# Four more tokens leave the dense expert tables and are gathered: 96 + 4 gathered, 160 to 156 dense

## The chip, the cores and the metric

One core of a Trainium2 chip runs the kernel. The metric is device time in microseconds; the figure shown of a kernel is the median of its runs.

## The reference, cut to what matters

A block over 256 tokens of width 2048: dilated attention and a three-branch sparse attention, a memory cross attention, and at the end a mixture over 16,384 small experts (PEER). Only the mixture and the last norm are touched here:

```python
eid = e1 * N_KEYS + e2
g = jax.nn.softmax(vs, axis=-1)
a = jax.nn.gelu(jnp.einsum('nd,ned->ne', xb, u_tab[eb]))
y = jnp.einsum('ne,ned->nd', a * gb, v_tab[eb])
h = h + y ; out = rmsnorm(h, norm_final)
```

Both tables `u_tab` and `v_tab` are 16384 x 2048 float32, 134 MB each.

## The kernel before, in words

`phase1` computes everything up to the first part of the query projection of the mixture. `phase2` is the mixture, and the change lies in it.

Tokens are handled in two ways. The first `NA` = 160 tokens are **dense**: both tables are streamed whole through TensorE, every expert is multiplied with all of these tokens, and a weight matrix that is zero where an expert wasn't chosen picks out what counts. Tokens 160 to 255 are **gathered**: an indirect DMA of GpSimd (POOL) fetches the 128 rows of a table that 128 partitions name, 1 MB a gather. `GROUPS` gives their layout: tokens 192 to 255 sit on 64 partitions, two copies of them, so that two experts of a token are fetched by one gather and 64 gathers do for a table; tokens 160 to 191 sit on 32 partitions, four copies, 32 gathers a table.

Order of the work:
- `route`, `give`, `gates` and `turned` find the experts and softmax weights, beside the query projection; `give` brings expert numbers and weights of the gathered tokens into the partition layout of their group by a matmul with a 0/1 matrix (`rep`), one quarter at a time (`b` = 0 to 3). `spread` builds the dense weight matrix from one-hot matmuls (`gp`, lines 1077 to 1105), one turn for four dense tokens, one turn in each tick.
- First table: 32 x 8 loads of 512 KB (line 1205) over the SP queue into eight buffers; a load feeds 8 matmuls of 128 x 128 by `NA` columns (line 1213), which the profile shows as 16 PE instructions, since float32 takes two each. In the text such a load with its matmuls is a **unit**.
- Second table: again 256 loads (line 1248) with 8 matmuls each (line 1242), summing into six PSUM banks over all 128 blocks of experts. The matmuls of blocks 126 and 127 are held back for the end (`close`).
- Gathers: the list `steps` holds them in order. `gtick` (line 1058) is called once a unit and moves on in the list by `RATE` = 0.415 steps a unit in the first table; at unit 256 the rate is set so that what is left is spent over 250 units of the second. Nine steps and the first are already done before, by `early` (line 1126) and line 1150. `paced` (line 985) ties each gather to the matmul that was the last when it was listed, so POOL goes no faster than TensorE. `fetch` takes one of four buffers `ga`; when three more are under way VectorE uses a fetched tile: `dot` (line 1010) against the token's row, `add` (line 1020) into the sum `acc`.
- `fold` (line 1030) adds up the copies of group 0 while the second table still runs: four matmuls of `acc` with a 0/1 matrix (line 1041) into two spare PSUM banks and four additions (line 1036). Group 1 is added up at the end, in `turn` (line 1280), which also transposes the dense result; then norm and output.

Tile orders each engine's instructions; TensorE, VectorE, ScalarE and POOL each work through their own queue in that order.

Of the kernel before, what the change touches and what calls it, by code (L numbers as in the profile page):

```python
# [26 lines left out]
A_SLOPES = [float(np.float32(2.0 ** (-8.0 * (i + 1) / 12))) for i in range(12)]  # L27
B_SLOPES = [float(np.float32(2.0 ** (-8.0 * (i + 1) / 16))) for i in range(16)]
ROW_NAMES = ("norm_mix", "norm_x", "norm_mem", "norm_ffn")
NA = 160  # L30
GROUPS = ((192, 64, 2), (160, 32, 4))
NE1 = 76
NPF = 7
GA = 4
LAG = 3
RATE = 0.415
SYNC = mybir.DependencyInfo(mybir.DependencyClass.Sync, mybir.DependencyReason.DATA)


# [814 lines left out]
def phase2(c):  # L854
    nc, I, pool = c.nc, c.I, c.pool
    g_s2, sp = pool("s2")
    g_ga, gap = pool("ga")
    g_w, wp = pool("wt")
    wta = wp.tile([128, NE1, NA], F32, name="wta")
    flat = wta[:].rearrange("p e n -> p (e n)")  # L860
    g_q, qp = pool("rt", side="right")
    skp = Banks(c.pp, ["s0", "s1"])
    up = Banks(c.pp, ["b0", "b1", "b2", "b3", "tr", "pv"])

    eT = [sp.tile([128, NA], F32, name=f"eT{i}") for i in range(3)]
    state = {"E": 0, "N": 0, "wtb": None, "unit": 0, "g": 0.0, "rate": RATE, "early": 0, "done": 0}
    selm = sp.tile([128, len(GROUPS), 128], F32, name="selm")
    nc.gpsimd.dma_start(selm[:], I["sel"])
    identr = qp.tile([128, 128], R, name="identr")
    nc.scalar.copy(identr[:], c.ident[:])  # L870
    sk = qp.tile([128, 2, 128], F32, name="sk")
    nc.gpsimd.dma_start(sk[:], I["sub_keys"])
    repk = qp.tile([128, sum(k for _, _, k in GROUPS), 128], F32, name="repk")
    nc.gpsimd.dma_start(repk[:], I["rep"])
    grp = []
    o = 0
    for gi, (t0, n, k) in enumerate(GROUPS):
        cc = 128 // k
        grp.append({"t0": t0, "n": n, "k": k, "cc": cc, "sum": selm[:, gi, :],
                    "rep": [repk[:, o + j, :] for j in range(k)],  # L880
                    "idx": sp.tile([128, cc], U32, name=f"idx{gi}"), "gate": sp.tile([128, cc], F32, name=f"gate{gi}"),
                    "a": sp.tile([128, cc], F32, name=f"a{gi}"), "rs": sp.tile([128, 1], F32, name=f"rs{gi}")})
        o += k
    v = qp.tile([128, 2, 16, 16], F32, name="v")
    ix = qp.tile([128, 2, 16, 16], U32, name="ix")
    ixk = qp.tile([128, 2, 16, 16], U32, name="ixk")
# [51 lines left out]
    def gates(hf, hs):  # L938

        n = hs.stop - hs.start  # L940
        gs = qp.tile([128, 2, 8], F32, name="gs")
        g3 = efs[hf][:, 2, 16 * hs.start:16 * hs.stop].rearrange("p (a c) -> p a c", c=16)
        v3 = vs[:, hf, hs, :]
        nc.vector.tensor_sub(g3, v3, v3[:, :, 0:1].to_broadcast([128, n, 16]))
        yield
        yield
        nc.scalar.activation(g3, g3, AF.Exp)
        yield
        nc.vector.reduce_sum(gs[:, 0, 0:n], g3, axis=AX.X)
        nc.vector.reciprocal(gs[:, 1, 0:n], gs[:, 0, 0:n])  # L950
        nc.vector.tensor_mul(g3, g3, gs[:, 1, 0:n][:, :, None].to_broadcast([128, n, 16]))

    def give(b):

        ef = efs[1]
        sl = slice(32 * b, 32 * b + 32)
        nc.vector.scalar_tensor_tensor(ef[:, 3, sl], ef[:, 0, sl], 128.0, ef[:, 1, sl], ALU.mult, ALU.add)
        yield from gates(1, slice(2 * b, 2 * b + 2))
        for _ in range(LAG):
            yield  # L960
        for g in grp:
            k, w = g["k"], 32 // g["k"]
            ps = skp.tile([128, 2, w], F32, name="sc")
            for j in range(k):
                nc.tensor.matmul(ps[:], g["rep"][j], ef[:, 2:4, 32 * b + j * w:32 * b + j * w + w],
                                 start=j == 0, stop=j == k - 1)
            nc.scalar.copy(g["gate"][:, b * w:b * w + w], ps[:, 0, :])
            nc.vector.tensor_copy(g["idx"][:, b * w:b * w + w], ps[:, 1, :])
            if b == 0:
                pr = skp.tile([128, 1], F32, name="sc")  # L970
                for j in range(k):
                    nc.tensor.matmul(pr[:], g["rep"][j], c.rsf[:, 1:2], start=j == 0, stop=j == k - 1)
                nc.scalar.copy(g["rs"][:], pr[:])
# [11 lines left out]
    def paced(ins):  # L985

        c.tc.add_manual_dep(ins.ins, c.last_sub.name, SYNC, reason="pace")

    def rows():
# [10 lines left out]
                nc.vector.scalar_tensor_tensor(g["x"][:], g["x"][:], g["rs"][:], gn[:], ALU.mult, ALU.mult)  # L1000
        return norm

    def fetch(g, i, table, use):
        t = gap.tile([128, D], F32, name="ga", tag="ga", bufs=GA)
        paced(nc.gpsimd.indirect_dma_start(out=t[:], out_offset=None, in_=table,  # L1005
                                           in_offset=bass.IndirectOffsetOnAxis(ap=g["idx"][:, i:i + 1], axis=0)))
        return lambda: use(g, i, t)
# [14 lines left out]
    steps = [rows]  # L1022
    for b in range(4):
        for g in grp:
            steps += [lambda g=g, i=i: fetch(g, i, I["ur"], dot) for i in range(b * g["cc"] // 4, (b + 1) * g["cc"] // 4)]
    for g in grp:
        steps += [lambda g=g, i=i: fetch(g, i, I["vr"], add) for i in range(g["cc"])]
    steps.insert(len(steps) - grp[1]["cc"] + 8, lambda: fold(grp[0]))

    def fold(g):  # L1030
# [7 lines left out]

    def share_sums(g, z, nb):
        r = slice(g["t0"] - 128, g["t0"] - 128 + g["n"])  # L1040
        nc.tensor.matmul(z[r, :], g["sum"][:, r], g["acc"][:, nb * 512:nb * 512 + 512], start=True, stop=True,
                         skip_group_check=True)
        return r

    def gathered():
# [93 lines left out]
    for b in range(4):  # L1139
# [58 lines left out]
    o = c.pj.n % 4  # L1198
    up.tags = ["tr", "pv"] + [f"b{(o + i) % 4}" for i in range(4)]
    for b in range(32):  # L1200
        e0 = 4 * b
        ps = [up.tile([128, 512], F32, name="up") for _ in range(4)]
        for u in range(8):
            i = 8 * b + u
            raw = ahead[i] if i < len(ahead) else load(I["u"][b, u])
            for k in range(2):
                kt = 2 * u + k
                x = xr[kt // 6][:, kt % 6, :]
                if b == 0:
# [59 lines left out]
    ss, rs = [fin[:, hf, 0:4] for hf in range(2)], [fin[:, hf, 5:6] for hf in range(2)]  # L1269
    n1 = NA - 128  # L1270
# [9 lines left out]
    def turn(nb):  # L1280
        zt = (spare, tags[0:2], tags[2:4], spare)[nb]
        z = [c.pp.tile([128, 512], F32, name=f"z{h}", tag=zt[h]) for h in range(2)]
        y = [ysb[d // 3][:, d % 3 * NA:d % 3 * NA + NA] for d in range(4 * nb, 4 * nb + 4)]
        for i in range(4):
            nc.tensor.transpose(z[0][:, i * 128:i * 128 + 128], y[i][:, 0:128], c.ident[:])
        for i in range(4):
            nc.tensor.matmul(z[1][0:n1, i * 128:i * 128 + 128], y[i][:, 128:NA], c.ident[:], start=i == 0, stop=True,
                             skip_group_check=True)
        share_sums(grp[1], z[1], nb)
        for hf in range(2):  # L1290
            x = hres[nb][:, hf, :]
            n = 128 if hf == 0 else GROUPS[0][0] - 128
            nc.vector.tensor_add(x[0:n], x[0:n], z[hf][0:n, :])
            nc.scalar.activation(sq[:, hf, :], x, AF.Square, accum_out=ss[hf][:, nb:nb + 1])

    def stat(hf):
# [135 lines left out]
```

## Time and profile before

| what | value |
|---|---|
| median of 3 runs | 2149.53 us (2148.39 to 2154.59) |
| profiled execution, its own time | 2152.23 us |
| its span | 2150.4 us |
| first table's matmuls (line 1213) | 915.8 to 1562.6 us |
| second table's matmuls (line 1242) | 1562.6 to 2135.1 us |
| moved by DMA | 642.15 MB, mean 299 GB/s |

A time is read as: engine busy, idle before, what ended the idle. `PEld` is the weight load of TensorE, beside `PE`, the matmuls. "DMA share" is the mean busy share of the 16 DMA engines, and can read a little over 1. Between the span and the execution's own time lie 1.8 us outside of the first and last instruction.

### The profile page before, as it was taken

The numbers are of one execution on the slowest core, as the hardware profiler recorded it, in microseconds if no ns is written. First come the engines' busy times: TensorE is split into PE (matmuls) and PEld (weight loads), VectorE is DVE, ScalarE is ACT, GpSimd is POOL, SyncE is SP. The second block draws the span as 40 slices with busy tenths as digits, with TensorE's granted clock in tenths as the row PEclk, the third lists the DMA queues.
The fourth block names the chain that finished last, engine by engine and source line by source line (L and its number), as shares of the span: only waits on it lengthen the run. The fifth ranks groups of instructions, "written<-read, shape, count | busy, mean of one in ns | idle before, by whom it ended". The sixth has DMA issues, their size and how long they took to land.

```text
span 2150.4 us, 36374 instructions
## 1 busy us (share of the span) xinstructions
PE 2109.8 (98%) x14602; PEld 1992.1 (93%) x14602; DVE 1236.1 (57%) x2304; ACT 565.3 (26%) x1290; POOL 272.0 (13%) x252
## 2 busy tenths in 40 slices
PE   8999999999999999999999999999999999999997
PEld 7998998777888888989989999999999999998996
DVE  5555655776575656798866666666443333333334
ACT  5454444656545555431101111000000000000001
POOL 0000000000000000132221221222311111111111
PEclk9999999999999999999999999999999999999999
DMA  7566545444655556888999999999999999998994
GB/s 247 177 193 190 166 137 165 147 138 138 195 177 188 186 168 218 262 309 337 397 414 415 407 401 407 405 399 408 414 413 413 412 412 404 400 385 320 397 394 189
DMA packets 152089, 642.15 MB, mean 299 GB/s; under 512 B 16928, under 2 KB 19264, under 8 KB 126960
## 3 DMA queue, kind: packets, MB, share of 16 engines
q1 hardware_dynamic: 120704, 426.06, 54.7%
q0 software_dynamic: 30496, 212.69, 24.8%
q8 instruction: 114, 1.87, 0.4%
q10 hardware_dynamic: 720, 1.08, 0.2%
q14 instruction: 55, 0.45, 0.1%
HBM read 635.57 MB, written 4.19 MB: 298 GB/s over the span
## 4 chain that ended last, share of the span: by engine, by line
PE 80%; issue 9%; DMA 5%; DVE 4%; POOL 2%; ACT 1%; POOLq 0%; DVEq 0%; ACTq 0%
PE up L1213 22%; PE y_b L1242 10%; PE pj L168 7%; PE pj L169 7%; PE pj L170 7%; PE y_s L1242 6%; PE pj L205 5%; PE pj L204 5%; PE pj L203 4%; DMA ga<-in_ur_dram,idx 2%; PE gp L1092 2%; POOL ga L1005 1%; DVE ga L1010 1%; DMA raw<-in_v_dram 1%; PE sc L602 1%
## 5 line engine op out<-in xcount | busy, mean ns | idle before, releaser
L1213 PE MATMUL up<-xr,raw 128*128 128x160 f32 x3968 | 547.3, 299 | 3.1 <-DMA raw<-in_u_dram 3.1
L150 DVE TENSOR_TENSOR wl<-raw,wh 128x512 fp32r<-128x512 f32 (+1 forms) x576 | 391.5, 684 | 268.1 <-ACT wh L149 265.3
L1213 PEld LDWEIGHTS up<-xr,raw 128*128 128x128 f32 x3968 | 540.5, 190 | 3.9 <-DMA raw<-in_u_dram 2.8
L149 ACT CAST wh<-raw 128x512 fp32r<-128x512 f32 (+1 forms) x576 | 352.0, 616 | 409.4 <-PE pj L204 166.4
L1020 DVE SCALAR_TENSOR_TENSOR acc<-ga,a,acc 128x2048 f32<-128x2048 f32 x94 | 221.0, 2352 | 397.6 <-DMA ga<-in_vr_dram,idx 397.6
L1010 DVE SCALAR_TENSOR_TENSOR ga<-ga,gx 128x2048 f32<-128x2048 f32 x96 | 219.9, 2291 | 148.9 <-DMA ga<-in_ur_dram,idx 148.8
L1242 PE MATMUL y_b<-wta,raw 128*128 128x160 f32 x1520 | 219.1, 299 | 0.6 <-DMA raw<-in_v_dram 0.6
L1242 PEld LDWEIGHTS y_b<-wta,raw 128*128 128x128 f32 x1520 | 210.6, 190 | 0.8 <-DMA raw<-in_v_dram 0.8
L1005 POOL DMA_INDIRECT ga<-in_vr_dram,idx x96 | 109.2, 1138 | 522.4 <-PE y_b L1242 440.8
L1005 POOL DMA_INDIRECT ga<-in_ur_dram,idx x96 | 125.8, 1310 | 378.7 <-PE up L1213 124.7
L205 PE MATMUL pj<-nh,wl 128*128 128x256 f32 x576 | 164.1, 285 | 0.0
L204 PE MATMUL pj<-nl,wh 128*128 128x256 f32 x576 | 164.0, 285 | 0.0
L203 PE MATMUL pj<-nh,wh 128*128 128x256 f32 x558 | 160.6, 288 | 0.0
L1242 PE MATMUL y_b<-wtb,raw 128*128 128x160 f32 x1040 | 151.8, 300 | 0.0
L168 PE MATMUL pj<-wh,nh 128*128 128x512 f32 (+1 forms) x384 | 150.2, 391 | 0.6 <-ACT wh L149 0.6
L1242 PEld LDWEIGHTS y_b<-wtb,raw 128*128 128x128 f32 x1040 | 144.6, 190 | 4.4 <-issue 4.4
L1278 ACT COPY ysb<-y_s 128x480 f32<-128x480 f32 x1 | 0.6, 560 | 560.0 <-PE y_s L1242 560.0
L169 PE MATMUL pj<-wl,nh 128*128 128x512 f32 (+1 forms) x384 | 147.2, 383 | 0.2 <-DVE wl L150 0.2
L170 PE MATMUL pj<-wh,nl 128*128 128x512 f32 (+1 forms) x384 | 147.0, 383 | 0.0
L1242 PE MATMUL y_s<-wta,raw 128*128 128x160 f32 x912 | 136.4, 299 | 0.2 <-DMA raw<-in_v_dram 0.2
L1242 PEld LDWEIGHTS y_s<-wta,raw 128*128 128x128 f32 x912 | 128.0, 190 | 0.4 <-DMA raw<-in_v_dram 0.4
L205 PEld LDWEIGHTS pj<-nh,wl 128*128 128x128 f32 x576 | 111.3, 193 | 0.7
(343 smaller groups left out, 2903.6 us busy)
## 6 DMA issues: line engine op xcount, KB each, us to landing
raw<-in_v_dram SPq DMA_DIRECT2D x256, 512.0 KB
raw<-in_u_dram SPq DMA_DIRECT2D x249, 512.0 KB
raw<-in_w_in_dram SPq DMA_DIRECT2D x160, 512.0 KB
raw<-in_w_out_dram SPq DMA_DIRECT2D x32, 512.0 KB
raw<-in_w_pq_dram SPq DMA_DIRECT2D x32, 512.0 KB
raw<-in_w_up_b_dram SPq DMA_DIRECT2D x16, 512.0 KB
raw<-in_w_xkv_dram SPq DMA_DIRECT2D x16, 512.0 KB
raw<-in_w_up_a_dram SPq DMA_DIRECT2D x8, 512.0 KB
```

The source lines that it names most:

```text
L149: c.last_act = nc.scalar.copy(h[:, :cols], raw[:, k, :cols]).ins
L150: c.last_sub = nc.vector.tensor_sub(l[:, :cols], raw[:, k, :cols], h[:, :cols].bitcast(F32)).ins
L168: nc.tensor.matmul(o, xh[:, s], h[:, :cols], start=kt == 0, stop=False)
L169: nc.tensor.matmul(o, xh[:, s], l[:, :cols], start=False, stop=False)
L170: c.last_mm = nc.tensor.matmul(o, xl[:, s], h[:, :cols], start=False, stop=kt == nk - 1).ins
L203: nc.tensor.matmul(o, h[:, s], xh, start=False, stop=False)
L204: nc.tensor.matmul(o, h[:, s], xl, start=False, stop=False)
L205: c.last_mm = nc.tensor.matmul(o, l[:, s], xh, start=False, stop=kt == nk - 1 and j % 2 == 1).ins
L1005: paced(nc.gpsimd.indirect_dma_start(out=t[:], out_offset=None, in_=table, in_offset=bass.IndirectOffsetOnAxis(ap=g["idx"][:, i:i + 1], ax ...
L1010: nc.vector.scalar_tensor_tensor(t[:], t[:], 1.0, g["x"][:], ALU.mult, ALU.mult, accum_out=g["a"][:, i:i + 1])
L1213: c.last_mm = c.last_sub = nc.tensor.matmul(ps[j][:, 0:NA], raw[:, k, j * 128:j * 128 + 128], x, start=kt == 0, stop=kt == KT - 1).ins
L1242: c.last_mm = c.last_sub = nc.tensor.matmul(o, raw[:, d // 4 % 2, d % 4 * 128:d % 4 * 128 + 128], wt, start=e == 0 and d % 3 == 0, stop=e ...
```

## The change

Tokens 156 to 159 leave the dense part (`NA` = 156) and are gathered as a third group, `four`: 4 tokens on 32 partitions each, so 4 gathers a table (128 partitions a gather, 32 experts of each token). Its rows `x` and its sum `acc` don't lie in one tile of 128 x 2048 but in four of 128 x 512, in buffers of the projection that are free by then. `give` gets a third layout step; `four_rows` loads the rows of the four tokens by 16 DMAs, each of which spreads 512 elements of one token over 32 partitions, and the gain row by one. `four_dot` and `four_add` do the work of `dot` and `add` in four pieces. In the list of steps, `four_rows` and the 4 gathers of the first table come behind the other 96, the 4 gathers of the second behind the first 8 of group 0, and a second `fold` stands five steps ahead of the first one. The rate in the first table goes from 0.415 to 0.395. In `turn` the second half's addition becomes two (partitions 0 to 27 and 32 to 63).

```diff
-NA = 160
+NA = 156
 GROUPS = ((192, 64, 2), (160, 32, 4))
+FOUR = 156
...
-RATE = 0.415
+RATE = 0.395
...
+    four = {"t0": 128, "n": 32, "cc": 4, "sum": selm[:, len(GROUPS), :], "rep": repk[:, o, :],
...
+        g = four
+        ps = skp.tile([128, 3, 32], F32, name="sc")
+        nc.tensor.matmul(ps[:, 0:2, :], g["rep"], ef[:, 2:4, sl], start=True, stop=True)
...
+        nc.vector.tensor_mul(own, ps[:, 0:2, :], g["mask"][:, None, :].to_broadcast([128, 2, 32]))
+        nc.vector.reduce_sum(g["gate"][:, b:b + 1], own[:, 0, :], axis=AX.X)
+        nc.vector.reduce_sum(own[:, 0, 0:1], own[:, 1, :], axis=AX.X)
+        nc.vector.tensor_copy(g["idx"][:, b:b + 1], own[:, 0, 0:1])
...
+    def four_rows():
...
+        for q in range(4):
+            for k in range(4):
+                paced(nc.gpsimd.dma_start(four["x"][q][32 * k:32 * k + 32, :],
+                                          c.h3[FOUR + k:FOUR + k + 1, q * 512:q * 512 + 512].to_broadcast([32, 512])))
+        paced(nc.gpsimd.dma_start(gn[:], I["norm_ffn"].to_broadcast([128, D])))
...
+    def four_dot(g, i, t):
+        for q in range(4):
+            s = t[:, q * 512:q * 512 + 512]
+            nc.vector.scalar_tensor_tensor(s, s, 1.0, g["x"][q][:], ALU.mult, ALU.mult, accum_out=g["part"][:, i, q:q + 1])
...
+    def four_add(g, i, t):
...
+        for q in range(4):
+            s, acc = t[:, q * 512:q * 512 + 512], g["acc"][q][:]
...
+                nc.vector.scalar_tensor_tensor(acc, s, g["a"][:, i:i + 1], acc, ALU.mult, ALU.add)
...
-    for g in grp:
-        steps += [lambda g=g, i=i: fetch(g, i, I["vr"], add) for i in range(g["cc"])]
+    steps.append(four_rows)
+    steps += [lambda i=i: fetch(four, i, I["ur"], four_dot) for i in range(4)]
+    steps += [lambda i=i: fetch(grp[0], i, I["vr"], add) for i in range(8)]
+    steps += [lambda i=i: fetch(four, i, I["vr"], four_add) for i in range(4)]
+    steps += [lambda i=i: fetch(grp[0], i, I["vr"], add) for i in range(8, grp[0]["cc"])]
+    steps += [lambda i=i: fetch(grp[1], i, I["vr"], add) for i in range(grp[1]["cc"])]
+    steps.insert(len(steps) - grp[1]["cc"] + 4, lambda: fold(four))
     steps.insert(len(steps) - grp[1]["cc"] + 8, lambda: fold(grp[0]))
...
-            n = 128 if hf == 0 else GROUPS[0][0] - 128
-            nc.vector.tensor_add(x[0:n], x[0:n], z[hf][0:n, :])
+            for r in ((slice(0, 128),), (slice(0, n1), slice(32, 64)))[hf]:
+                nc.vector.tensor_add(x[r], x[r], z[hf][r, :])
```

## Rows read from the trace of the kernel before

**Rows 1.** The page: busy time, share of the span and instructions of each engine; the costliest group of the first table (line engine op, out<-in, count | busy, mean ns of one | idle before, what ended it); the two DMA queues that carry the mixture, loads first and gathers second (packets, MB, share).

```profile
PE 2109.8 (98%) x14602; PEld 1992.1 (93%) x14602; DVE 1236.1 (57%) x2304; ACT 565.3 (26%) x1290; POOL 272.0 (13%) x252
L1213 PE MATMUL up<-xr,raw 128*128 128x160 f32 x3968 | 547.3, 299 | 3.1 <-DMA raw<-in_u_dram 3.1
q1 hardware_dynamic: 120704, 426.06, 54.7%
q0 software_dynamic: 30496, 212.69, 24.8%
```


**Rows 2.** Windows of the tables, all engines: stretch in us, its length, busy us (instructions) of PE, PEld, DVE, ACT and POOL, the granted clock, the DMA share and the GB/s moved. First table with and without `gp` turns, second table early and later, the one stretch in which TensorE starved, and two stretches of the query projection.

```profile
1200.00:1504.00 304.00, 304.00 (x2283) 304.00 (x2282) 198.50 (x445) 29.27 (x171) 65.06 (x54) 1.00 1.01 404
1504.00:1562.00 58.00, 58.00 (x429) 58.00 (x429) 28.04 (x25) 3.52 (x13) 19.57 (x11) 1.00 1.02 414
1562.00:1762.00 200.00, 199.26 (x1465) 198.78 (x1464) 71.55 (x35) 1.12 (x4) 32.31 (x35) 1.00 1.02 413
1762.00:1930.00 168.00, 168.00 (x1239) 168.00 (x1238) 55.37 (x24) 0.00 (x0) 26.74 (x25) 1.00 1.01 399
1072.00:1096.00 24.00, 20.91 (x150) 20.01 (x149) 16.72 (x20) 2.39 (x11) 5.72 (x5) 1.00 1.02 419
900.00:920.00 20.00, 19.42 (x161) 19.09 (x161) 18.12 (x60) 8.17 (x17) 6.05 (x5) 1.00 0.71 246
920.00:960.00 40.00, 36.66 (x294) 35.44 (x294) 36.35 (x102) 15.00 (x31) 12.31 (x7) 1.00 0.87 299
```


**Rows 3.** Timeline of PE: start, length, line, operation, tile shape and count of a run of back-to-back instructions, for 160 columns and for 128; then the group of the 128-column ones, with the mean ns of one ahead of the last bar.

```profile
1306.69 11.03 PE L1213 MATMUL up<-xr,raw 128*128 128x160 f32 x80
906.45 1.95 PE L1156 MATMUL sc<-sk,qt 128*128 128x128 f32 x16
L1156 PE MATMUL sc<-sk,qt 128*128 128x128 f32 x48 | 5.8, 275 | 0.0
```


**Rows 4.** Waits (who waited for whom: us in total, times, longest): TensorE for loads from 900 to 1110 us, and from 1562 to 1938 us; the SP queue from 1000 us on, which waits until TensorE frees a buffer. Then a piece of the chain of waits: start, us, the load that TensorE waited for.

```profile
PE up L1213 <- DMA raw<-in_u_dram: 3.1, 3, 1.3
PE y_b L1242 <- DMA raw<-in_v_dram: 0.6, 1, 0.6
PE y_s L1242 <- DMA raw<-in_v_dram: 0.2, 1, 0.2
SPq L1192 <- PE y_b L1242: 444.5, 247, 8.3
1652.04 15.30 DMA raw<-in_v_dram
```


**Rows 5.** Gathers by POOL, grouped by line from 1562 us to the end, and then the last gather and the last accumulation in the timeline.

```profile
L1005 POOL DMA_INDIRECT ga<-in_vr_dram,idx x78 | 81.6, 1046 | 451.3 <-PE y_b L1242 440.8 <-issue 7.0 <-PE up L1213 3.4
2109.34 0.94 POOL L1005 DMA_INDIRECT ga<-in_vr_dram,idx  x1 [5.58 <-PE y_b L1242]
2117.76 2.35 DVE L1020 SCALAR_TENSOR_TENSOR acc<-ga,a,acc 128x2048 f32<-128x2048 f32 x1 [3.43 <-DMA ga<-in_vr_dram,idx]
```


**Rows 6.** Timeline of the one fold, about 1936 us: PEld and PE of its matmuls, the normal matmuls between them, VectorE's work, and the first normal run after it.

```profile
1935.74 0.19 PEld L1041 LDWEIGHTS zf<-acc,selm 128*64 128x64 f32 x2 [0.17 <-issue]
1935.75 1.93 PE L1041 MATMUL zf<-acc,selm 128*64 128x512 f32 x4
1937.61 1.90 PE L1242 MATMUL y_b<-wtb,raw 128*128 128x160 f32 x12
1938.33 2.35 DVE L1020 SCALAR_TENSOR_TENSOR acc<-ga,a,acc 128x2048 f32<-128x2048 f32 x1 [4.18 <-DMA ga<-in_vr_dram,idx]
1940.71 1.30 DVE L1036 TENSOR_TENSOR wta<-wta,zf 64x512 f32<-64x512 f32 x2
1941.46 1.73 PE L1041 MATMUL zf<-acc,selm 128*64 128x512 f32 x2 [1.95 <-DVE wta L1036]
1943.12 1.44 PE L1242 MATMUL y_b<-wtb,raw 128*128 128x160 f32 x4
1944.48 1.39 PE L1041 MATMUL zf<-acc,selm 128*64 128x512 f32 x2
1945.80 1.90 PE L1242 MATMUL y_s<-wtb,raw 128*128 128x160 f32 x12
```


**Rows 7.** What comes nearest to the new pieces: the row loads of the two groups by POOL (six and one), and a product and a sum of VectorE on 128 columns, in which the last number ahead of the second bar is the mean ns.

```profile
864.27 3.00 POOL L995 DMA_DIRECT2D gx<-h  x6 [13.17 <-DVE wl L150]
867.26 0.56 POOL L996 DMA_DIRECT2D ga<-in_norm_ffn_dram  x1
L951 DVE TENSOR_TENSOR ef<-ef,gs 128x128 f32<-128x128 f32 x1 | 0.3, 291 | 0.0
L949 DVE TENSOR_REDUCE gs<-ef 128x8 f32<-128x128 f32 x1 | 0.3, 282 | 0.0
```


**Rows 8.** The end: the last `turn` (matmul of group 1's sum, the two additions) and what follows on VectorE.

```profile
2137.12 0.59 PE L1041 MATMUL z<-acc,selm 128*32 128x512 f32 x1
2136.31 0.69 DVE L1293 TENSOR_TENSOR wta<-wta,z 128x512 f32<-128x512 f32 x1 [0.75 <-PE z L1285]
2137.75 0.68 DVE L1293 TENSOR_TENSOR wta<-wta,z 64x512 f32<-64x512 f32 x1 [0.76 <-PE z L1041]
2138.36 0.14 DVE L1298 TENSOR_REDUCE fin<-fin 128x1 f32<-128x4 f32 x1
```

More of the change, by code (lines that the diff above doesn't have):

```diff
@@ L866, in phase2 @@
     state = {"E": 0, "N": 0, "wtb": None, "unit": 0, "g": 0.0, "rate": RATE, "early": 0, "done": 0}
-    selm = sp.tile([128, len(GROUPS), 128], F32, name="selm")
+    selm = sp.tile([128, len(GROUPS) + 1, 128], F32, name="selm")
     nc.gpsimd.dma_start(selm[:], I["sel"])
@@ L872, in phase2 @@
     nc.gpsimd.dma_start(sk[:], I["sub_keys"])
-    repk = qp.tile([128, sum(k for _, _, k in GROUPS), 128], F32, name="repk")
+    repk = qp.tile([128, sum(k for _, _, k in GROUPS) + 1, 128], F32, name="repk")
     nc.gpsimd.dma_start(repk[:], I["rep"])
@@ L883, in phase2 @@
         o += k
+    four = {"t0": 128, "n": 32, "cc": 4, "sum": selm[:, len(GROUPS), :], "rep": repk[:, o, :],
+            "mask": qp.tile([128, 32], F32, name="mask4"), "idx": sp.tile([128, 4], U32, name="idx4"),
+            "gate": sp.tile([128, 4], F32, name="gate4"), "a": sp.tile([128, 4], F32, name="a4"),
+            "part": sp.tile([128, 4, 4], F32, name="part4"), "rs": sp.tile([128, 1], F32, name="rs4")}
+    nc.vector.reduce_sum(four["mask"][:], c.ident[:].rearrange("p (t a) -> p a t", t=4), axis=AX.X)
     v = qp.tile([128, 2, 16, 16], F32, name="v")
@@ L973, in give @@
                 nc.scalar.copy(g["rs"][:], pr[:])
+        g = four
+        ps = skp.tile([128, 3, 32], F32, name="sc")
+        nc.tensor.matmul(ps[:, 0:2, :], g["rep"], ef[:, 2:4, sl], start=True, stop=True)
+        own = qp.tile([128, 256], F32, name="tmp", bufs=2)[:, 0:64].rearrange("p (a b) -> p a b", a=2)
+        nc.vector.tensor_mul(own, ps[:, 0:2, :], g["mask"][:, None, :].to_broadcast([128, 2, 32]))
+        nc.vector.reduce_sum(g["gate"][:, b:b + 1], own[:, 0, :], axis=AX.X)
+        nc.vector.reduce_sum(own[:, 0, 0:1], own[:, 1, :], axis=AX.X)
+        nc.vector.tensor_copy(g["idx"][:, b:b + 1], own[:, 0, 0:1])
+        if b == 0:
+            nc.tensor.matmul(ps[:, 2, 0:1], g["rep"], c.rsf[:, 1:2], start=True, stop=True)
+            nc.scalar.copy(g["rs"][:], ps[:, 2, 0:1])
         yield
@@ L1001, in rows, with norm @@
         return norm
+    def four_rows():
+        gn = gap.tile([128, D], F32, name="ga", tag="ga", bufs=GA)
+        four["x"] = [c.hlp.tile([128, 512], F32, name="x4", tag="wh") for _ in range(4)]
+        for q in range(4):
[3 more added lines that the diff above has]
+        paced(nc.gpsimd.dma_start(gn[:], I["norm_ffn"].to_broadcast([128, D])))
+        def norm():
+            for q in range(4):
+                x = four["x"][q]
+                nc.vector.scalar_tensor_tensor(x[:], x[:], four["rs"][:], gn[:, q * 512:q * 512 + 512], ALU.mult, ALU.mult)
+        return norm
+    def four_dot(g, i, t):
+        for q in range(4):
+            s = t[:, q * 512:q * 512 + 512]
+            nc.vector.scalar_tensor_tensor(s, s, 1.0, g["x"][q][:], ALU.mult, ALU.mult, accum_out=g["part"][:, i, q:q + 1])
+        if i == 3:
+            nc.vector.reduce_sum(g["a"][:], g["part"][:], axis=AX.X)
+            nc.scalar.activation(g["a"][:], g["a"][:], AF.Gelu_apprx_tanh)
+            nc.vector.tensor_mul(g["a"][:], g["a"][:], g["gate"][:])
+    def four_add(g, i, t):
+        if i == 0:
+            g["acc"] = [c.hlp.tile([128, 512], F32, name="acc4", tag="wl") for _ in range(4)]
+        for q in range(4):
+            s, acc = t[:, q * 512:q * 512 + 512], g["acc"][q][:]
+            if i == 0:
+                nc.vector.tensor_scalar_mul(acc, s, g["a"][:, 0:1])
+            else:
+                nc.vector.scalar_tensor_tensor(acc, s, g["a"][:, i:i + 1], acc, ALU.mult, ALU.add)
     def fetch(g, i, table, use):
@@ L1040, in share_sums @@
         r = slice(g["t0"] - 128, g["t0"] - 128 + g["n"])
-        nc.tensor.matmul(z[r, :], g["sum"][:, r], g["acc"][:, nb * 512:nb * 512 + 512], start=True, stop=True,
-                         skip_group_check=True)
+        a = g["acc"]
+        nc.tensor.matmul(z[r, :], g["sum"][:, r], a[nb][:] if isinstance(a, list) else a[:, nb * 512:nb * 512 + 512],
+                         start=True, stop=True, skip_group_check=True)
         return r
@@ L1381, in selections @@
         rep += [(row[:, None] == t0 - 128 + row[None, :] % n) & (row[None, :] // n == j) for j in range(k)]
+    four = FOUR - 128 + row // 32
+    sums.append(four[:, None] == row[None, :])
+    rep.append(row[:, None] == four[None, :])
     return [np.stack(a, 1).astype(np.float32) for a in (sums, rep)]
```

## The prediction

> **What bounds the kernel now.** Read the page first [rows 1]: TensorE is busy 98% of the span, and the two tables take 915.8 to 2135 us of it. That alone would say that fewer dense columns are time gained. So look second at the windows, DMA column [rows 2]: with `gp` turns the first table moves 404 GB/s at a share of 1.01, without them 414; the second table 413 for its first 200 us and 399 later. Third, how much more there is: from 1072 to 1096 us TensorE starved (20.9 of 24 us busy, waiting for loads [rows 4]), and the engines moved 419. So 413 to 419 GB/s is what DMA gives when all is asked of it, and the kernel sits 1 to 4% under that. Fourth, the waits [rows 4]: SP waits 444.5 us for TensorE to free a buffer, so TensorE sets the pace, but at 1652 us one load took 15.3 us, seven units, and TensorE waited for it. **TensorE is the bound by a hair; DMA stands right behind it.**
>
> **A unit of TensorE.** 80 instructions of 160 columns take 11.03 us; without the last one's 0.299 us that is 10.73/79 = 0.1358 us each [rows 1, 3]. At 128 columns: (1.95-0.275)/15 = 0.1117. The slope is 0.75 ns a column, so four columns are worth 3.0 ns; in plain proportion of 0.1358 they are 3.4. I take 3.2. A unit of 16 goes from 2.173 to 2.122 us. A table is 256 units, 4096 instructions: **-13.1 us a table** (12.3 to 13.9), if TensorE remains the bound. One of 40 `gp` turns goes too: 8 instructions of 0.112, -0.9.
>
> **First table.** Bytes: a load is 0.524 MB, a gather 1.049 MB. A unit asks for 0.524+0.415x1.049 = 0.960 MB before, 0.524+0.395x1.049 = 0.939 after, 2.2% less; the unit is 2.3% shorter. So the demand stays at the 404 GB/s of before [rows 2], below 413, and the saving stands: -14.0. Against it:
> - `give` in four turns, each with two small matmuls, one product, two sums and a copy on VectorE. On 128 columns a product is 0.291 and a sum 0.282 us [rows 7]; on 32 to 64 some 0.2, so 0.8 a turn. The stage has VectorE at 18.1 of 20 and 36.4 of 40 us busy [rows 2], so most is not hidden: +1.5 for the three turns in the projection (0 to 3).
> - `four_rows`: 17 DMAs at the 0.5 to 0.56 us of the existing ones [rows 7] hold POOL 9 us, against a gather each 2.5 units or 5.8 us. Two gathers queue behind it, nobody needs them soon. Its 2.1 MB stand in the place of one gather's 1.05, at a point where demand is already 414: 1.05/415 = 2.5 us of DMA, half of it on the path, +1.3 (0 to 2.5). The Trainium skill speaks against such pieces ("DMA: Bandwidth & Descriptors", section Bandwidth): it gives a 64 KB transfer 0.95 us. By it the sixteen pieces hold DMA 15.2 us, an estimate, and the sum below would be up to 14 us higher; no row here shows such a piece.
>
> First table: **-11.2**.
>
> **Second table.** Here the bytes go up. Before, the list has 194 steps; 79 (78 gathers, one fold) are in the second table [rows 5], 0.316 a unit. After, it has 1+96+1+4+64+4+32 and two folds = 204. The first table does floor(255x0.395) = 100, ten come earlier, and 94 remain: 92 gathers and two folds, 94/250 = 0.376 a unit. A unit asks 0.524+0.376x1.049 = 0.919 MB; in 2.122 us that is **433 GB/s, more than any window shows**. DMA becomes the bound here. The list puts the new fold as the 65th of those steps, unit 173.
> - Until then: 173x0.919 = 158.9 MB, and 3.15 MB for the residual and gain (six DMAs of 512 KB, lines 1257 and 1259): 162.1 MB. At 415 GB/s (between the 413 and the 419) 390.5 us. Before, the same 173 units took 376.0 and 0.7 of waits: +13.8 (+10.2 at 419, +15.8 at 413). Loads don't start with a reserve: the 58 us ahead of the second table ask more than they get, and the load at 1652 us shows it used up. Gathers may lag by up to the four buffers that they have, which puts off 0 to 2.5 MB: -1.5 (0 to -6).
> - After it the folds' pauses fill the eight buffers; 83 units fall short by 0.919-2.122x0.415 = 0.038 MB each, 3.2 MB, which the buffers cover: TensorE's pace, -4.2.
> - The fold of `four`: the existing one takes from 1935.7 to 1945.8, in which 16 normal instructions are 2.2 us: 7.9 us, because its additions stand behind an accumulation on VectorE and TensorE waits for the bank [rows 6]. Without these waits it is 8 instructions of some 0.43, 3.4 us. I take +5.
> - VectorE's four pieces instead of one 2.35 us operation are hidden: VectorE is busy 71.6 of 200 us.
>
> Second table: **+13.1**.
>
> **The end.** In each `turn` one addition more, 0.68 us [rows 8]; surely on the path in the last, partly in the others: **+1.4** (0.7 to 2.7).
>
> **Sum:** -11.2+13.1+1.4 = +3.3 on the profiled execution's 2152.2, so 2155.5. That execution lies 2.7 above the median; against the median, 2152.8: **2153 us**, no change. What can be told from no change here is about 0.3%, 6.4 us. With all terms at their low ends: -14.8+10.2-6-4.5+3.4+0.7 = -11; at their high ends -13.2+5.5+15.8-4.0+7.9+2.7 = +14.7. Its own range, as not all ends come together: 2143 to 2162.
>
> **Rivals.**
> 1. *DMA gives what is asked.* Where 419 is not the ceiling, the second table stays at TensorE's pace: -11.2-13.1+5+1.4 = -17.9, 2132. For it: no window of before asks 433, so none can show it. Against: from 1072 to 1096 us TensorE stood waiting, and it was still 419. The Trainium skill ("DMA: Bandwidth & Descriptors", Specifications) puts the fabric's ceiling at 435 GB/s; by that the 433 would just fit, and this rival would be the case. The 419 of the starved stretch speaks against it. Chance 0.18.
> 2. *The first table is DMA bound too, slower.* If the 404 GB/s at a share of 1.01 is not what was asked but what the mix allows, the second table gets about 406: 162.1/0.406 = 399.3 us, +22.6 in place of +13.8, and the first gives back some 3 us: +3.3+8.8+3+1.5 (no lag helps) = +16.6, 2166. It decides from a rate under 409 on. For it: the share column makes no difference between 404 and 414. Against: TensorE doesn't wait for a load in that stretch, and right after it 414 was moved. Chance 0.12.
> 3. *Gathers pile up at the end, slower.* Now the last gather starts at 2109.3, its accumulation ends at 2120.1 [rows 5], some 4 us ahead of its use. If gathers lag by all four buffers, 4.2 MB are still to come, 10 us, of which 6 are over: +3.3+6 = +9.3, 2159. For it: 0.376 gathers a unit against 0.316. Against: after the folds DMA has room. Chance 0.10.
> 4. *The change doesn't do what it says:* the dense instruction doesn't get shorter with its columns. Rows of 160 and 128 differ [rows 3], so this is left at no chance of its own.
>
> **How the numbers follow.** Forecast 0.60. Range: 2139 to 2165, which leaves out most of rival 1 (0.14), and the upper part of rival 2 (0.06). Faster by over 0.3% (under 2143): rival 1, 0.18. Slower (over 2156): rivals 2 and 3, 0.22, and 0.3 of the forecast's own spread, 0.18: 0.40. The same: 0.42.
>
> **What would show it.** Right: in the first table a unit of 16 instructions near 2.12 us and 404 GB/s; in the second until about 1940 us a flat 413 to 419, TensorE waiting for loads there, some 22 us in all (389 less 173x2.122) where now it is 0.8; two dips of the folds, and 2.12 a unit behind them. Wrong: over 425 GB/s in the second table (rival 1); waits for loads in the first table after 1110 us (rival 2); VectorE still accumulating when the last matmul of block 125 is done (rival 3). A second table not longer than before would fell the forecast's main term.

## The result, and the profile after

The changed kernel takes 2174.89 us (median; 2169.98 to 2181.19), the kernel before 2150.99 beside it: ratio **1.0106, 95% interval 1.0092 to 1.0120**, 23 us slower. The forecast was 2153 (2139 to 2165). The profiled execution is a high one, 2181.19 us; its span is 2179.4, 29.0 more than before's.

The page: the engines' line, the first table's main group, the gathers' queue, as in [rows 1].

```profile
PE 2105.1 (97%) x14612; PEld 1971.6 (90%) x14612; DVE 1263.6 (58%) x2374; ACT 563.8 (26%) x1290; POOL 309.3 (14%) x277
L1271 PE MATMUL up<-xr,raw 128*128 128x156 f32 x3968 | 538.6, 297 | 9.6 <-DMA raw<-in_u_dram 8.3 <-ACT gl L1281 1.3
q0 software_dynamic: 32320, 223.31, 25.6%
```

TensorE has less work and is busy a smaller share; its waits for loads in the first table rise from 3.1 to 8.3 us; the gathers' queue carries 10.62 MB more. The windows that answer to [rows 2]:

```profile
1202.00:1504.00 302.00, 302.00 (x2317) 302.00 (x2317) 190.47 (x440) 28.90 (x170) 59.14 (x68) 1.00 1.01 400
1504.00:1562.00 58.00, 52.62 (x388) 51.34 (x387) 29.41 (x57) 3.09 (x13) 12.07 (x10) 1.00 1.02 414
1562.00:1762.00 200.00, 189.03 (x1388) 184.31 (x1387) 78.63 (x49) 1.10 (x4) 49.49 (x39) 1.00 1.02 413
1762.00:1930.00 168.00, 160.93 (x1187) 157.65 (x1187) 65.84 (x28) 0.00 (x0) 42.20 (x29) 1.00 1.02 414
1930.00:2040.00 110.00, 103.34 (x707) 93.97 (x706) 37.08 (x22) 0.00 (x0) 17.22 (x15) 0.97 0.87 342
2040.00:2120.00 80.00, 79.41 (x599) 79.17 (x599) 32.92 (x14) 0.00 (x0) 24.71 (x15) 1.00 1.02 414
```

Read the last column downwards: 413 to 414 GB/s from 1504 on, with TensorE now idle 5.5% of the time from 1504 to 1930, but 342 in the stretch of the two folds; what isn't moved there is missing afterwards, where 2040 to 2120 runs at 414. Before, with one fold, the last two stretches were:

```profile
1930.00:2040.00 110.00, 108.05 (x760) 103.41 (x760) 35.61 (x18) 0.00 (x0) 14.59 (x15) 0.98 0.92 357
2040.00:2120.00 80.00, 80.00 (x591) 80.00 (x590) 28.10 (x12) 0.00 (x0) 12.17 (x11) 1.00 0.97 380
```

The instruction itself did what was priced. A run of 64 in the first table, and the waits on loads in the second table up to the first fold (before: 0.6 and 0.2 [rows 4]):

```profile
1301.66 8.65 PE L1271 MATMUL up<-xr,raw 128*128 128x156 f32 x64
PE y_b L1300 <- DMA raw<-in_v_dram: 9.5, 17, 1.1
PE y_s L1300 <- DMA raw<-in_v_dram: 8.5, 12, 1.5
```

(8.65-0.297)/63 = 0.1326 us, 3.2 ns less than 0.1358. The new fold, beside [rows 6]:

```profile
1951.69 1.90 PE L1099 MATMUL zf<-acc,selm 128*32 128x512 f32 x4
1953.53 1.86 PE L1300 MATMUL y_s<-wtb,raw 128*128 128x156 f32 x12
1955.22 0.69 PE L1300 MATMUL y_b<-wtb,raw 128*128 128x156 f32 x4
1959.51 3.40 PE L1099 MATMUL zf<-acc,selm 128*32 128x512 f32 x4 [3.59 <-DVE wta L1093]
...
1956.51 2.35 DVE L1072 SCALAR_TENSOR_TENSOR acc<-ga,a,acc 128x2048 f32<-128x2048 f32 x1 [3.88 <-DMA ga<-in_vr_dram,idx]
1958.78 1.27 DVE L1093 TENSOR_TENSOR wta<-wta,zf 32x512 f32<-32x512 f32 x2
```

11.15 us from 1951.69 to 1962.84 with 16 normal instructions (2.12) in them: 9.0 lost. VectorE's additions stand behind an accumulation that waits 3.88 us for its gather. Around each fold POOL issues no gather for over 18 us; from 1963 to 1966 the DMA engines moved nothing at all, while TensorE was busy throughout:

```profile
1967.62 0.94 POOL L1057 DMA_INDIRECT ga<-in_vr_dram,idx  x1 [18.89 <-PE y_b L1300]
2003.81 0.94 POOL L1057 DMA_INDIRECT ga<-in_vr_dram,idx  x1 [18.29 <-PE y_b L1300]
```

Where 29 us came from, in three stretches cut at events that every kernel has: the first dense instruction, the first `gp` matmul (unit 59), the first of the second table, the end of the span. All profiled runs but the one at rate 0.412, means in us:

| profiles | to `gp` | `gp` to second table | second table to end |
|---|---|---|---|
| 160 columns, no gathers added (5) | 183.6 | 465.6 | 586.9 |
| 160 columns, ten gathers twice (1) | 180.4 | 464.2 | 604.2 |
| 156 columns alone (1) | 190.7 | 459.1 | 578.7 |
| 156 columns, ten gathers twice (1) | 182.3 | 454.3 | 608.4 |
| the changed kernel (1) | 185.8 | 459.4 | 616.5 |
| it and its variants at rate 0.395 (8) | 182.1 | 460.4 | 601.8 to 617.9 |

The first stretch scatters by 10 us between executions, so one profile tells little of it; the second table takes 585.5 to 588.1 in the five of the first row.

### The profile page after: what moved, and what is told of

Read it like the earlier page. It is cut to its first block, busy times and chain, and to the rows that moved or that the text cites. A ratio compares the mean times of both kernels' runs of the same rounds, so it can differ in the third digit from the quotient of the medians.

```text
span 2179.4 us, 36513 instructions
## 1 busy us (share of the span) xinstructions
PE 2105.1 (97%) x14612; PEld 1971.6 (90%) x14612; DVE 1263.6 (58%) x2374; ACT 563.8 (26%) x1290; POOL 309.3 (14%) x277
## 4 chain that ended last, share of the span: by engine, by line
PE 70%; DMA 13%; issue 10%; DVE 3%; POOL 3%; ACT 1%; POOLq 0%; DVEq 0%; ACTq 0%
PE up L1271 22%; DMA raw<-in_v_dram 7%; PE pj L169 7%; PE pj L170 7%; PE pj L171 7%; PE pj L206 4%; PE y_b L1300 4%; PE pj L205 4%; PE pj L204 4%; POOL ga L1057 3%; PE y_s L1300 3%; DMA raw<-in_u_dram 2%; PE gp L1150 2%; DMA raw<-in_w_pq_dram 1%; DMA ga<-in_ur_dram,idx 1%
## 5 line engine op out<-in xcount | busy, mean ns | idle before, releaser
L1271 PE MATMUL up<-xr,raw 128*128 128x156 f32 x3968 | 538.6, 297 | 9.6 <-DMA raw<-in_u_dram 8.3
L1271 PEld LDWEIGHTS up<-xr,raw 128*128 128x128 f32 x3968 | 530.5, 191 | 12.0 <-DMA raw<-in_u_dram 6.7
L1300 PE MATMUL y_b<-wta,raw 128*128 128x156 f32 x1520 | 219.2, 297 | 9.8 <-DMA raw<-in_v_dram 9.5
L1057 POOL DMA_INDIRECT ga<-in_vr_dram,idx x100 | 143.2, 1432 | 471.9 <-PE y_b L1300 411.0
L1057 POOL DMA_INDIRECT ga<-in_ur_dram,idx x100 | 120.1, 1201 | 432.1 <-PE up L1271 148.3
L1300 PE MATMUL y_b<-wtb,raw 128*128 128x156 f32 x1040 | 149.0, 298 | 0.7 <-DMA raw<-in_v_dram 0.7
L1300 PE MATMUL y_s<-wta,raw 128*128 128x156 f32 x912 | 134.8, 298 | 6.5 <-DMA raw<-in_v_dram 6.3
```

What stands on the lines that cost most here:

```text
L1300: c.last_mm = c.last_sub = nc.tensor.matmul(o, raw[:, d // 4 % 2, d % 4 * 128:d % 4 * 128 + 128], wt, start=e == 0 and d % 3 == 0, stop=e ...
```

## The experiments

Ratios are to the kernel before, run on the same chip.

**Bytes or instructions.** The shorter instruction alone: the changed kernel without `four`.

```diff
-    steps.append(four_rows)
-    steps += [lambda i=i: fetch(four, i, I["ur"], four_dot) for i in range(4)]
...
-RATE = 0.395
+RATE = 0.415
```

> The dense part alone: 156 columns, and the four tokens 156 to 159 get no expert sum at all (left out: their gathers, rows, dots, sums and folds; the rate is 0.415 again). It moves the bytes of the kernel before. If TensorE is the bound in both tables (34.0 us less work in them by the step of 3.3 ns an instruction, 26 of it on the path), about 2125. If the loads are the bound everywhere, within 4 us of the kernel before (2147 to 2151). If the first table is TensorE's until the loads reach 414 GB/s and the second is the loads' already, 13 to 18 us less than before (2133 to 2138).

Measured: 2140.39 us, 0.9941 (0.9924 to 0.9957), 12.7 us of the 26 that 8192 instructions by 3.2 ns make (the 34 of the expectation was a slip of mine). Something else already caps half of TensorE's gain, and not only the loads: in its profile, the slowest of its six executions, TensorE waits 7.4 us for the first one-hots, 5.5 us for VectorE's routing ahead of them and 2.5 us for loads in the first table, which gains nothing, while the second gains 8. Now the bytes alone, on the kernel before:

```diff
+        if b == 3:
+            steps += [lambda i=i: fetch(grp[0], i, I["ur"], dot) for i in range(10)]
```

> The kernel before, 160 columns, with ten gathers of the first table done twice (same indices, same sums) and the rate 0.395: +10.5 MB, the bytes that the change adds, with no new kind of row, gelu, fold or give. Bytes theory (the loads are the bound): 10.5 MB at 413 GB/s, +25 us, 2174 to 2178. Stall theory (the loss of the change is its new waits): some bytes hide beside TensorE, +10 to +16 us, 2161 to 2167. If TensorE were the bound everywhere: within 5 us of before.

Measured: 2169.60, 1.0080 (1.0058 to 1.0102), +17 us. Between the theories: some bytes hide beside 160 columns. And the same ten lines on the 156 columns:

> 156 dense columns without the four tokens (their expert sums are left out), and ten gathers of the first table done twice, rate 0.395: the shorter instructions and the bytes of the change together, without its rows, gelu, give and second fold. If the two edits' times add, the -13.5 us of the one and the +15.7 us of the other give 2156. If with the shorter instructions the loads are the bound, so that the bytes cost their full 25 us, 2140 + 25 = 2165, and what the changed kernel has over that (some 10 us) is its new waits. If the new waits cost nothing: 2174 to 2178.

Measured: 2164.28, 1.0070 (1.0050 to 1.0089). **The edits don't add**: the same bytes cost 17 us at 160 columns and 28 at 156, about what 10.5 MB take at 413 GB/s (25.4). Each cost is uncertain by some 5 us (by the medians they are 16 and 24), and the difference of 11 by some 7: it is clear of noise, but not by much. Windows from its second table:

```profile
1560.00:1920.00 360.00, 343.48 (x2526) 335.65 (x2526) 139.54 (x60) 0.00 (x0) 98.65 (x65) 1.00 1.02 413
1920.00:2040.00 120.00, 115.70 (x828) 110.33 (x827) 44.17 (x23) 0.00 (x0) 20.06 (x18) 0.99 0.96 385
2040.00:2120.00 80.00, 78.49 (x586) 77.51 (x585) 32.50 (x15) 0.00 (x0) 19.81 (x14) 1.00 1.02 414
```

The same 413 as in the changed kernel: 15 of the 23 us are there with the change's columns and bytes alone. The other 7 to 8, uncertain by some 5, are looked for in the rest of this section.

**The new waits.** In `give` one PSUM tile for all groups (not shown), and the line with the gelu of `four` later:

```diff
-        if i == 3:
-            nc.vector.reduce_sum(g["a"][:], g["part"][:], axis=AX.X)
-            nc.scalar.activation(g["a"][:], g["a"][:], AF.Gelu_apprx_tanh)
...
+        if i == 0:
+            nc.scalar.activation(g["a"][:], g["a"][:], AF.Gelu_apprx_tanh)
```

> The changed kernel with two of its new waits taken away: give does the products of all its groups into one PSUM tile before any of them is copied out, and the gelu of the four's dots stands at their first accumulation instead of behind their last dot, so that ScalarE's queue doesn't stand behind a gather. Stall theory: about 5.6 us of TensorE in give and about 6 us behind the gelu come back, 2161 to 2166. Bytes theory (the loads are the bound, what TensorE loses in one place it has to wait for elsewhere anyway): within 3 us of the changed kernel, 2172 to 2177.

Measured: 2177.21, 1.0112 (1.0088 to 1.0136): nothing. The wait in `give` (2.7 us in the changed kernel's profile) was gone, and TensorE waited 6.5 us at the first `gp` for one-hots instead. The gelu, though, did not move: the line stands elsewhere in the program, but in ScalarE's queue the operation kept its place right behind the last dot's sum. ScalarE idle ahead of it, in the changed kernel and in this one:

```profile
1527.05 0.21 ACT L1042 ACTIVATE a<-a 128x4 f32<-128x4 f32 x1 [21.30 <-DVE a L1041]
1522.81 0.20 ACT L1055 ACTIVATE a<-a 128x4 f32<-128x4 f32 x1 [20.50 <-DVE a L1051]
```

So this run tests the wait in `give` alone, and the kernels built on it have two of the three waits taken away, not three: in two of them TensorE still waits 2.4 and 3.0 us for ScalarE. Next, on the changed kernel, the folds copied out by ScalarE, in two steps each:

```diff
-            nc.vector.tensor_add(x, x, z[r, :])
+            nc.scalar.copy(zs[r, :], z[r, :])
+            nc.vector.tensor_add(x, x, zs[r, :])
```

> The changed kernel with both folds' PSUM tiles copied out by ScalarE and added from SBUF, each fold in two steps, so that TensorE doesn't wait for VectorE's adds behind a late gather. Stall theory: of some 17 us in the two folds about 10 come back, 2163 to 2168. Bytes theory: the loads that stand in the folds are made up only in part, within 4 us of the changed kernel, 2171 to 2176.

Measured: 2170.11, 1.0089 (1.0063 to 1.0115), some 4 us, which the intervals don't part from nothing; no wait at a fold is left, and the profile's second table is 609.8. All these edits together (below called `all_fixed`), and then with the rate raised to 0.412:

> The changed kernel with its three waits taken away together: one PSUM tile in give, the four's gelu at their first accumulation, both folds copied out by ScalarE in two steps each. If waits add what they lose alone (give and gelu 0, folds 6): 2170. If the two only show together, since a stall that goes in the first table is late again at the fold: 2163 to 2167. Bytes theory: not under the 2165 of the run with 156 columns and ten more gathers.

> The kernel with the three waits taken away and the rate 0.412 in place of 0.395: some four gathers (4.2 MB, 10 us of loads at 413 GB/s) come in the first table instead of the second. If both tables are bound by the loads, the sum is the same: within 3 us of the run at 0.395. If the first table is still TensorE's and only the second the loads', 4 to 8 us less. If the first table is more bound by loads than the second, slower.

Measured: 2171.48, 1.0101 (1.0079 to 1.0123), and 2172.71, 1.0104 (1.0084 to 1.0124). At 0.412 the second table is 603.6 instead of 611.0, and the first 651.4 instead of 640.9; 8.1 us of that are the wait for the first one-hots (12.4 in place of 4.3). Nothing is won by moving bytes between the tables. That fits two tables at the cap, but it doesn't show it of the first, which runs at 401 to 407 GB/s while `gp` turns go on.

**The folds' empty steps.** A fold is a step in the gathers' list, so in its turn no gather goes. Issue it together with one, in the changed kernel (`no_slot`) and in `all_fixed` (`all_fixed_no_slot`):

```diff
-    steps.insert(len(steps) - grp[1]["cc"] + 4, lambda: fold(four))
-    steps.insert(len(steps) - grp[1]["cc"] + 8, lambda: fold(grp[0]))
+    also(len(steps) - grp[1]["cc"] + 4, four)
+    also(len(steps) - grp[1]["cc"] + 8, grp[0])
```

> The changed kernel, with each fold issued in the step of a gather instead of in a step of its own, so that no step of the second table goes without a gather; nothing else. Theory of the empty step: in the 12 to 19 us that the two folds leave without a gather the load buffers are full, the DMA engines move 348 GB/s where the stretches around move 413, and 5 to 8 us of bytes are late at the end: 2167 to 2170. Theory that the folds cost their waits on TensorE alone: within 2 us of the changed kernel (2173 to 2177).

> The kernel with the three waits taken away (2171.5), where its four fold steps leave four steps without a gather and 1920 to 2040 moves 369 GB/s; here the halves of the folds go with a gather's step. Theory of the empty step: 6 to 9 us less, 2162 to 2166, and over 400 GB/s in 1920 to 2040. If the loss there is not the empty steps: 2169 to 2173.

Measured: 2173.79, 1.0112 (1.0091 to 1.0133), and **2163.42, 1.0071 (1.0044 to 1.0097)**. Alone it gives nothing: with a gather closer in front of the additions TensorE's wait at the folds rose from 6.2 to 9.9 us. With the folds' waits gone it gives 8 us by the medians, 6.5 by the ratios. The intervals of the ratios overlap, but the profiles agree: from 1920 to 2040 the changed kernel moves 348 GB/s, `no_slot` 348, `all_fixed` 369 and `all_fixed_no_slot` 398; their second tables take 616.5, 617.9, 611.0 and 601.8 us. Windows of `all_fixed`, then of `all_fixed_no_slot`:

```profile
1920.00:1960.00 40.00, 39.37 (x273) 35.61 (x271) 13.09 (x9) 2.30 (x4) 7.54 (x5) 1.00 0.96 373
1960.00:2000.00 40.00, 40.00 (x281) 36.88 (x280) 12.08 (x8) 2.33 (x4) 3.82 (x5) 1.00 0.88 331
2000.00:2040.00 40.00, 40.00 (x304) 40.00 (x303) 16.38 (x7) 0.00 (x0) 8.89 (x7) 1.00 1.01 404
```

```profile
1920.00:1960.00 40.00, 39.21 (x284) 37.25 (x283) 15.96 (x9) 1.15 (x2) 8.54 (x6) 1.00 1.02 413
1960.00:2000.00 40.00, 40.00 (x269) 35.24 (x268) 18.51 (x14) 3.48 (x6) 5.88 (x6) 1.00 0.97 377
2000.00:2040.00 40.00, 40.00 (x304) 40.00 (x303) 14.14 (x6) 0.00 (x0) 8.32 (x7) 1.00 1.01 403
```

Its ratio is that of the 156 columns with ten more gathers (1.0070), but this is in part luck, for the profiles differ: its first table is 7.2 us longer (643.8 beside 636.6), its second 6.6 us shorter (601.8 beside 608.4), since that kernel still has an empty step of its one fold. So the equal totals don't show that only bytes are left.

**The rows of the four.** While the 16 pieces of 64 KB go, the changed kernel moves a quarter less, at a share of 1.03 to 1.05 (its windows from 1488):

```profile
1488.00:1492.00 4.00, 4.00 (x33) 4.00 (x32) 1.74 (x1) 0.00 (x0) 1.72 (x5) 1.00 1.03 312
1492.00:1496.00 4.00, 4.00 (x33) 4.00 (x32) 3.06 (x13) 0.34 (x2) 2.42 (x6) 1.00 1.05 293
1496.00:1500.00 4.00, 4.00 (x33) 4.00 (x33) 0.69 (x2) 0.21 (x1) 2.18 (x4) 1.00 1.05 282
1500.00:1504.00 4.00, 4.00 (x32) 4.00 (x31) 0.00 (x0) 0.00 (x0) 1.76 (x3) 1.00 1.04 303
```

297.5 on average; (414-297.5) x 16 us = 1.86 MB, 4.5 us. Is it the size of the pieces, or the one row that 32 partitions read? On `all_fixed`, four pieces of 8 KB a partition, and then with 32 different rows each:

```diff
-                paced(nc.gpsimd.dma_start(four["x"][q][32 * k:32 * k + 32, :],
+            paced(nc.gpsimd.dma_start(xr[32 * k:32 * k + 32, :],
```

> The changed kernel with the three waits taken away, and the four tokens' rows read by 4 DMAs of 32 partitions by 8 KB into one gather buffer in place of 16 DMAs of 32 partitions by 2 KB; the same 1 MB. The changed kernel moves 282 to 312 GB/s for 16 us while the 16 go (DMA share 1.05), 413 before and after. If the 2 KB pieces are what slows the queues, that stretch comes to 400 GB/s or more and 4 us of the 7 that the three-waits kernel is over the 156 columns with ten more gathers go: 2166 to 2168. If it is that 32 partitions read the same row, it stays near 300 GB/s and 2170 to 2173.

> The kernel with the rows by 4 DMAs of 8 KB, but each of the four reads 32 different rows of the same tensor in place of one row 32 times (the four tokens' rows are replaced by those of other tokens). If reading one row 32 times is what slows the queues to 244 to 255 GB/s for 8 us, the stretch moves 400 GB/s or more here. If it is that a transfer goes to 32 partitions only, it stays under 300 GB/s. The time is one look: 2166 to 2176.

Measured: 2175.24, 1.0114 (1.0091 to 1.0138), and 2174.66 in a single run. Windows from 1488 of the first, and from 1484 of the second:

```profile
1488.00:1492.00 4.00, 4.00 (x32) 4.00 (x31) 2.22 (x3) 0.00 (x0) 0.87 (x1) 1.00 1.06 244
1492.00:1496.00 4.00, 4.00 (x33) 4.00 (x32) 2.58 (x13) 0.34 (x2) 1.57 (x2) 1.00 1.01 255
```

```profile
1484.00:1488.00 4.00, 4.00 (x34) 4.00 (x33) 0.97 (x5) 0.44 (x4) 0.83 (x2) 1.00 1.06 327
1488.00:1492.00 4.00, 4.00 (x32) 4.00 (x32) 3.67 (x9) 0.34 (x2) 2.04 (x1) 1.00 1.02 236
1492.00:1496.00 4.00, 4.00 (x33) 4.00 (x32) 1.12 (x5) 0.00 (x0) 0.96 (x1) 1.00 1.01 336
```

1.3 and 1.4 MB short: neither the 2 KB pieces nor the one row read 32 times is the cause of all of it. What all three have in common is that a transfer goes to 32 partitions and reads `h`; the same rows in one transfer to 128 partitions weren't tried, so the cause stays open. (The gain row, sent to 128 partitions behind them, isn't it: in the changed kernel it lands at 1508.2, and from 1504 on the mix is back at 419.) No time came back: in the first of the two TensorE is busy 36.4 of the 40 us from 1480, 39.3 in `all_fixed`. Perhaps the second gather buffer that the row tile takes is why; no run parts the two.

**A kernel faster than both?** Three tries on the kernel before: the fold copied out by ScalarE, this at rate 0.395, and no gather's step around the first one-hots; the rate alone as a control.

```diff
+        if not state.get("hold"):
             state["g"] += state["rate"]
```

> The kernel before with its fold copied out by ScalarE and added from SBUF, in two steps. The fold keeps TensorE 7.9 us from its products, of which 4 x 0.95 us are the fold's own: if TensorE is the bound of the second table, 2 to 4 us less than before (2150 to 2152 beside 2153.9). If the loads bound it, nothing (within 2 us).

> The kernel before with its fold copied out by ScalarE, and the rate 0.395: five gathers fewer in the first table, five more in the second, where its DMA engines had 16 to 25 us of room. If TensorE bounds both tables and what the first loses is the wait for one-hots behind a gather: 3 to 6 us less than the same kernel at 0.415, 2143 to 2147. If the bytes moved cost in the second what they free in the first: within 2 us of it (2148 to 2151).

> The kernel before with the rate 0.395 alone: parts the rate from the fold. If the rate is worth 3 to 6 us by itself: 2146 to 2149. If it only moves bytes between the tables: within 2 us of before.

> The kernel before with its fold copied out by ScalarE, and no gather's step issued from the three units ahead of the one-hots' start until their first four tokens are done: VectorE has fewer dots that wait for a gather in front of the first one-hots, for which TensorE waited 1.8 to 12.4 us in the profiles so far. If that wait is TensorE's loss in the first table: 2 to 5 us less than the fold alone, 2145 to 2148, and the wait under 2 us. If the loads bound the stretch, the wait goes and TensorE waits for raw instead: within 2 us.

Measured: 2149.57, 0.9988 (0.9973 to 1.0003); 2152.57, 1.0005 (0.9994 to 1.0016); 2153.65, 1.0008 (0.9997 to 1.0019); 2152.96, 1.0005 (0.9991 to 1.0018). None is faster, and the hold missed for a reason worth seeing. VectorE and TensorE of that run, at the first one-hots:

```profile
1091.73 2.29 DVE L1010 SCALAR_TENSOR_TENSOR ga<-ga,gx 128x2048 f32<-128x2048 f32 x1 [1.45 <-DMA ga<-in_ur_dram,idx]
1095.51 2.29 DVE L1010 SCALAR_TENSOR_TENSOR ga<-ga,gx 128x2048 f32<-128x2048 f32 x1 [1.48 <-DMA ga<-in_ur_dram,idx]
1097.73 0.67 DVE L1093 TENSOR_SCALAR oh<-iota,eT 128x128 f32<-128x128 f32 x3
...
1090.36 1.80 PE L1222 MATMUL up<-xr,raw 128*128 128x160 f32 x12
1098.80 2.05 PE L1096 MATMUL gp<-oh,oh 128*128 128x128 f32 x8 [6.64 <-DVE oh L1094]
```

The gathers of the dots in front were issued earlier, the last at 1083.51, ahead of the hold, and land one each 3.75 us or so. The one-hots start at 1097.73 whatever TensorE does (before: 1097.47, with TensorE there at 1096.8 and a wait of 1.8). TensorE came sooner and waited longer.

## Why the prediction was wrong, step by step

- *A unit, 2.173 to 2.122 us*: right (3.2 ns an instruction).
- *First table, -11.2* (the step "the demand stays at the 404 GB/s of before [rows 2], below 413, and the saving stands: -14.0"): failed. The changed profile gained 1.7; over the profiles at rate 0.395 183.6 + 465.6 become 182.1 + 460.4, -6.7. The first 59 units, priced at -3.0, gave nothing that stands out of the scatter. In 12 of the 17 profiles TensorE waits there for the first one-hots, 1.8 to 12.4 us, which a shorter instruction doesn't move, as they stand behind dots behind gathers; in the changed kernel's own it waits for loads (4.2), `give` (2.7) and ScalarE (1.8) instead. This I read from the traces, as no run took the dots away. Units 100 to 228 gave all that was priced (296.4 us beside 304.1). It was lost in the last 28, mostly behind the last `gp` turn: 67.1 us, beside 61.7 before and 60.3 in the 156 columns with ten more gathers. In the changed profile TensorE there waits 4.1 us for loads and 1.3 for ScalarE, whose queue stood 21.3 us behind the gelu of `four`, while that kernel waits for neither.

  The step took the rate of the stretch with `gp` turns for the whole table: by its own figures a unit without them asks 0.939 MB in 2.122 us, 442 GB/s, more than the 433 that made DMA the bound of the second table. I had priced `four_rows` at 1.3; its slow stretch alone is 4.5 us of bytes. That it makes the waits behind it is argued, as no run took it away alone. The Trainium skill ("DMA: Bandwidth & Descriptors", Bandwidth) gives a 64 KB transfer 0.95 us, by which the estimate was up to 14 us for the sixteen. The 4.5 measured beside other traffic are less, but the direction was right, and I had let it count for nothing.
- *Second table until the new fold, +12.3 with the lag*: the mechanism right, the size too small. To the fold it is 388.7 us in place of 373.0, but the fold comes one unit sooner (170 units are done, 171 before); the same 170 units took 370.7 before, so it is +18.0, over the +10.2 to +15.8 allowed. The rate was 413 to 414 GB/s as thought, near the low bound; the lag of gathers that was to help (-1.5) isn't seen, for 160.6 MB were moved by then where 159.4 were reckoned. TensorE waited 18.0 us for loads where 22 were forecast.
- *After it: "the folds' pauses fill the eight buffers ... which the buffers cover: TensorE's pace, -4.2", and the fold +5, the end +1.4*: failed. From unit 170 to the end 227.8 in place of 216.9 us, +10.9 where +2.2 was forecast. The end itself was right (+0.8). The new fold took 9.0, the old one 8 as before, now with a wait of 2.57. And the buffers don't cover the rest: once they are full the loads stop, and as the fold's step sends no gather the DMA engines have nothing to move (342 GB/s from 1930 to 2040). TensorE waits 3.6 us more for loads between the first fold and the end. Waits and empty steps together are the likely cause: with the folds' waits and the empty steps both taken away the ratio falls from 1.0106 to 1.0071, 7.5 us (uncertain by some 6); either alone gives nothing clear of noise, -1 to 4 us.
- *The sum, +3.3*: the three measured parts, -1.7, +18.0 and +10.9, add to some +27, and the first dense instruction comes 1.9 later already (917.8 against 915.9): 29.0, the spans' difference.
- *Rivals.* 1 (DMA gives what is asked, 2132) is out: with 433 GB/s asked for, no stretch of 200 us moved over 414, in any run; 40 us reach 416, 4 us 434. The Trainium skill ("DMA: Bandwidth & Descriptors", Specifications) puts the fabric's ceiling at 435 GB/s; no run here sustains it. 2 (the first table bound by DMA too, 2166) is right that DMA binds at that table's end, not in the rate: 414 GB/s were moved there, not 406. Of 3 (gathers pile up at the end) nothing was seen.

The error was to price each edit where it stands. Before, TensorE was late by a hair and hid the 1 to 4% by which DMA ran under its 413; the change spent that slack twice, once on a shorter instruction, once on bytes.

## What to carry to other kernels

Where two resources are within a few per cent, add up the work of each over the whole stage and take the larger sum; a saving on the one buys at most the slack of the other, and an added byte then costs about its full time (17 us at 160 columns, 28 at 156). A rate averaged over a stage hides the part of it in which the demand is over the cap (here the last 28 units of the first table). A stall of TensorE beside DMA that is saturated before and after isn't repaid by full buffers: keep transfers going through it. Before pricing a faster engine, look for the next point where it meets a queue that it doesn't drive (here VectorE, paced by gathers), for time saved ahead of such a point may be lost there; the traces here suggest it, and no run shows it. And look in the trace whether an edit moved the operation: the gelu's line moved, and the gelu didn't.

## What the runs showed of the hardware

- 413 to 414 GB/s at a share of 1.02 is what this mix of 512 KB loads and gathers gets over 200 us when all is asked for, in every kernel here; 40 us windows reach 416, 4 us windows 434 (the changed kernel from 1072, the kernel before at rate 0.395 from 1586).
- Transfers of 64 or 256 KB to 32 partitions that read `h` bring the mix down to 236 to 336 GB/s in 4 us windows, while the DMA engines stay fully busy (share 1.01 to 1.06). Whether the 32 partitions or `h` is the cause wasn't parted.
- Six executions of nearly one first table at 160 columns ended it between 1557.9 and 1568.5 us. Most of the scatter arises ahead of unit 59 (the first `gp` between 1093.7 and 1102.0): the three that ended last waited 6.6 to 7.6 us for the one-hots there, the other three 0 to 1.8.
